# A two-layer hybrid decoder trunk on one core: the tile scheduler draws up the instruction order with its timeline machine model

## Chip, cores and metric

One core of one Trainium2 chip runs the whole kernel in one launch. The metric is the time on the device in microseconds (us), the median of several executions of the same program. Beside it stands one profiled execution, whose trace gives the start and the length of every instruction. Engines are named as in the profile: PE is TensorE's matmul, PEld its weight load, DVE is VectorE, ACT is ScalarE, POOL is GpSimd, SP is SyncE, which here issues every DMA. "SPq" is SP's queue of DMA issues.

## The reference

Sequence 1024, width 1024, batch 1, all float32. Layer 0 is retention with 4 heads, layer 1 is stick-breaking attention with 8 heads over a shared K and V.

```python
u = rms_norm(h, ret_norm_pre);  q, k, v, g = split(u @ ret_w_in)
q, k = rope(q), rope(k) * QK ** -0.5
o = retention_chunkwise(q, k, v)          # o_t = sum_{s<=t} gamma^(t-s) (q_t.k_s) v_s
o = layer_normalised(o) * silu(g)
h = h + rms_norm(o @ ret_w_out, ret_norm_post)
k_sh, v_sh = split(rms_norm(h, kv_norm) @ w_kv)
q, g = split(rms_norm(h, sb_norm_pre) @ sb_w_in)
o = stick_breaking(q, k_sh, v_sh) * silu(g)   # A = sigmoid(z) * prod of (1 - sigmoid(z)) between
h = h + rms_norm(o @ sb_w_out, sb_norm_post)
```

## The kernel before

The function `trunk` writes out the whole computation, transposed, with no loop at run time. The sequence is cut into two halves of 512 tokens, and the work runs through four phases: layer 0 on half 0, layer 0 on half 1, layer 1 on half 0, layer 1 on half 1. A phase has four units: a retention head (`AHead`) or a pair of attention heads (`CPair`).

Every product of float32 operands is done as three matmuls (`mm3`, lines 110 to 112) of operands that are split into a high and a low part. `split` makes the parts: ACT writes the high part (line 262, or 265 with a gain), then DVE writes the low part (line 263, or 266). Weights go through this too. `unit` loads a weight block of 128x1024 in two halves into buffers `wraw` (6 of 128x512) and splits it into `whl` (3 of 128x2x1024). A projection (`proj`) walks over 4 such weight blocks in 16 chunks of 6 matmuls each, so one weight block feeds 24 matmuls of 512 columns, and the next block is requested (`get(kk + 1)`) while the present one is used. Results gather in PSUM tiles `pma` and `pmb` (2 each); transposes and scores use `pz` (2), attention sums `po` (2).

The order in which the code issues its steps is written by hand: `merge` takes a main list (projection chunks) and side lists (scores, attention sums, gates, norms) and spreads the side steps over the main ones.

```python
def merge(main, *sides, nxt=None):
    done = [0] * len(sides)
    for i, m in enumerate(main):
        ...
        m()
        for k, (steps, lead, tail) in enumerate(sides):
            n = len(main) - lead - tail
            upto = min(len(steps), len(steps) * max(0, i + 1 - lead) // n)
            while done[k] < upto:
                steps[done[k]]()
                ...
```

That is not yet the order in which the engines run. When the block `with tile.TileContext(nc) as tc:` closes, the tile framework's scheduler runs the traced instructions through a model of the machine. Whenever an engine of the model is free, the scheduler gives it the earliest instruction in code order whose operands and buffers are ready in the model. It also hands out the buffers of each tag in that process, and puts in the semaphore waits. Each engine then runs its list strictly in that order on the chip; nothing is chosen again at run time. Without an argument the model is the framework's core simulator.

In the program that comes out before the change, TensorE's list has 8094 matmuls and transposes and steps back in code order at 8 places only. The other lists are far from code order already: DVE's 1947 instructions step back 505 times, ACT's 1526 324 times, SP's 1055 DMAs 196 times, POOL's 374 15 times.

Other lines that the prediction speaks of: 64 (every DMA's issue), 202 (`outproj` adds to a stored partial sum `y`), 504 and 508 (the sums of a product with seven multiplications in `vg`, which also forms sums of weights in lines 480 to 489), 694, 702 and 703 (`a_post`: residual add on POOL or DVE, square on ACT, sum on POOL), 806 (the gate's SiLU), 961 to 983 (`finish`, the last norm and the output).

## Time and profile before

| | |
|---|---|
| time, 3 runs | 1782.42, 1786.29 and 1787.54 us, median 1786.29 |
| profiled execution, first to last instruction | 1779.2 us |
| time of the profiled execution itself | not listed; by the three runs it lies 3.2 to 8.3 us above the span |
| instructions recorded | 23669 |
| PE, DVE, ACT, POOL busy | 97%, 67%, 46%, 16% of the span |
| mean granted TensorE clock | 0.996 of full speed |
| moved by DMA | 292.14 MB, mean 164 GB/s |

Busy time is the union of an engine's instructions; matmuls are pipelined, so their recorded lengths overlap, and what a stretch achieves is read better from the count of matmuls in it.

### The profile page before, as it was taken

The page shows a single profiled execution, that of the slowest core. Times are in us where ns is not written, and L with a number is a line of the kernel's source. Part 1 is how long each engine was busy: PE and PEld are TensorE (multiplying, and loading weights), DVE is VectorE, ACT ScalarE, POOL GpSimd, SP SyncE. Part 2 cuts the span into 40 slices and gives each one's busy share as a digit, 9 for nine tenths or more (in the row PEclk, how much of TensorE's full clock was granted, in tenths as well). Part 3 has the DMA queues.
Part 4 walks back from the last instruction along what each step waited for, and adds up shares of the span by engine and source line. Part 5 has one row for each costly group of instructions (what it writes and reads, how often), then busy time and mean ns, then how long its engine had stood idle before and what let it go on. Part 6 is the DMA issues. An engine that isn't in the chain of part 4 may idle for free.

```text
span 1779.2 us, 23669 instructions
## 1 busy us (share of the span) xinstructions
PE 1732.0 (97%) x8132; PEld 1432.3 (81%) x8132; DVE 1198.6 (67%) x1947; ACT 815.1 (46%) x1526; POOL 290.2 (16%) x377
## 2 busy tenths in 40 slices
PE   8999999999999999999999999999999999999997
PEld 6888788777788788877887888888778888888886
DVE  7756767789766868697485455556677456656675
ACT  6435545455445535364344343444445434444441
POOL 0210412232304320111130100000200010000003
PEclk9999999999999999999999999999999999999999
DMA  5225465557445646275664526345644433522243
GB/s 192 84 101 195 153 236 173 193 179 271 168 143 189 226 144 233 97 258 187 230 222 159 194 95 204 117 151 173 221 135 158 140 131 103 179 94 99 95 137 113
DMA packets 152553, 292.14 MB, mean 164 GB/s; under 512 B 17136, under 2 KB 19312, under 8 KB 152432
## 3 DMA queue, kind: packets, MB, share of 16 engines
q1 hardware_dynamic: 152432, 290.63, 48.2%
q8 instruction: 64, 1.05, 0.2%
q14 instruction: 57, 0.47, 0.1%
HBM read 233.93 MB, written 56.62 MB: 163 GB/s over the span
## 4 chain that ended last, share of the span: by engine, by line
PE 42%; issue 27%; DVE 16%; DMA 7%; POOL 4%; ACT 3%; SPq 1%; POOLq 0%; DVEq 0%; ACTq 0%
PE pma L111 6%; PE pmb L110 6%; PE pmb L111 6%; PE pmb L112 6%; PE pma L112 6%; PE pma L110 6%; DVE whl L263 3%; DMA wraw<-in_wts_dram 3%; PE po L111 2%; PE po L112 2%; PE po L110 2%; DVE sgn L838 1%; POOL small L622 1%; DMA y<-f 1%; DMA S<-in_xT_dram 1%
## 5 line engine op out<-in xcount | busy, mean ns | idle before, releaser
L263 DVE TENSOR_TENSOR whl<-wraw,whl 128x512 fp32r<-128x512 f32 x312 | 220.5, 735 | 67.8 <-ACT whl L262 67.2
L266 DVE SCALAR_TENSOR_TENSOR whl<-wraw,gn,whl 128x256 fp32r<-128x256 f32 (+1 forms) x256 | 153.5, 643 | 127.7 <-ACT whl L265 124.9
L262 ACT ACTIVATE whl<-wraw 128x512 fp32r<-128x512 f32 x312 | 183.5, 624 | 111.5 <-PE pmb L112 52.4
L265 ACT ACTIVATE whl<-wraw,gn 128x256 fp32r<-128x256 f32 (+1 forms) x256 | 143.1, 612 | 166.3 <-PE pmb L112 135.7
L110 PE MATMUL pmb<-xh,whl 128*128 128x512 f32 x384 | 153.1, 399 | 2.8 <-DVE sg L806 2.6
L110 PE MATMUL pma<-xh,whl 128*128 128x512 f32 x384 | 153.3, 399 | 1.2 <-DVE v L263 0.7
L112 PE MATMUL pmb<-xh,whl 128*128 128x512 f32 x384 | 150.3, 391 | 0.0
L112 PE MATMUL pma<-xh,whl 128*128 128x512 f32 x384 | 150.2, 391 | 0.0
L111 PE MATMUL pma<-xh,whl 128*128 128x512 f32 x384 | 149.8, 390 | 0.0
L111 PE MATMUL pmb<-xh,whl 128*128 128x512 f32 x384 | 149.7, 390 | 0.0
L836 POOL TENSOR_SCALAR_AFFINE_SELECT sgn<-sgn 128x128 f32<-128x128 f32 x64 | 24.8, 387 | 692.0 <-ACT sgn L831 580.1
L838 DVE TENSOR_TENSOR_SCAN sgn<-sgn 128x128 f32<-128x128 f32 (+3 forms) x64 | 89.1, 1393 | 45.0 <-POOL sgn L836 45.0
L263 DVE TENSOR_TENSOR AT<-pz,AT 128x512 fp32r<-128x512 f32 (+1 forms) x96 | 53.0, 553 | 72.3 <-ACT AT L262 71.9
L262 ACT ACTIVATE AT<-pz 128x512 fp32r<-128x512 f32 (+1 forms) x96 | 46.7, 487 | 111.5 <-PE pz L868 108.9
L110 PEld LDWEIGHTS pmb<-xh,whl 128*128 128x128 f32 x384 | 72.2, 188 | 18.5 <-DVE sg L806 5.3
L112 PEld LDWEIGHTS pmb<-xh,whl 128*128 128x128 f32 x384 | 72.1, 188 | 15.8
L112 PEld LDWEIGHTS pma<-xh,whl 128*128 128x128 f32 x384 | 72.1, 188 | 15.6
L110 PEld LDWEIGHTS pma<-xh,whl 128*128 128x128 f32 x384 | 72.2, 188 | 15.0 <-DVE v L263 1.1
L111 PEld LDWEIGHTS pmb<-xh,whl 128*128 128x128 f32 x384 | 72.2, 188 | 13.4
L111 PEld LDWEIGHTS pma<-xh,whl 128*128 128x128 f32 x384 | 72.3, 188 | 13.0
L110 PE MATMUL pma<-oT,whl 128*128 128x512 f32 x208 | 82.2, 395 | 0.5 <-DVE small L619 0.5
L111 PE MATMUL pma<-oT,whl 128*128 128x512 f32 x208 | 81.4, 392 | 1.2 <-DVE oT L263 1.2
(321 smaller groups left out, 4507.4 us busy)
## 6 DMA issues: line engine op xcount, KB each, us to landing
wraw<-in_wts_dram SPq DMA_DIRECT2D x624, 256.0 KB, 3.2
y<-f SPq DMA_DIRECT2D x120, 256.0 KB, 3.2
f<-y SPq DMA_DIRECT2D x88, 256.0 KB, 3.8
v<-v SPq DMA_DIRECT2D x16, 512.0 KB, 3.3
vo<-v SPq DMA_DIRECT2D x32, 256.0 KB, 2.9
A<-h SPq DMA_DIRECT2D x12, 512.0 KB, 4.3
st<-ko SPq DMA_DIRECT2D x8, 512.0 KB, 3.9
sg<-in_xT_dram SPq DMA_DIRECT2D x16, 256.0 KB, 2.9
```

What stands on the lines that cost most here:

```text
L110: MM(p, lh, rh, start=start, stop=False, **kw)
L111: MM(p, lh, rl, start=False, stop=False, **kw)
L112: MM(p, ll, rh, start=False, stop=stop, **kw)
L262: A_.activation(dst[0], src, AF.Copy)
L263: V.tensor_tensor(dst[1], src, f32(dst[0]), ALU.subtract)
L265: A_.activation(dst[0], src, AF.Copy, scale=scale)
L266: V.scalar_tensor_tensor(dst[1], src, scale, f32(dst[0]), ALU.mult, ALU.subtract)
L622: G.tensor_tensor(r[:], r[:], mhalf[:, 0:1], ALU.pow)
L836: G.affine_select(n[:, dg], n[:, dg], [[-1, 128]], ALU.is_gt, 1.0, base=0, channel_multiplier=1)
L838: V.tensor_tensor_scan(n[:, :W][:, ::-1], n[:, :W][:, ::-1], n[:, :W][:, ::-1], 1.0, ALU.mult, ALU.bypass)
```

## The change

The scheduler's machine model is replaced: it now runs the traced instructions through the framework's timeline simulator, which models each engine's sequencer, queue and data path, the DMA engines and the semaphores' travel as separate devices. No instruction of the computation, no tile, buffer count or hint in the code differs. All five instruction lists, TensorE's among them, are drawn up anew, as are the buffers that each tile gets and the semaphore waits that follow from the order.

```diff
-    with tile.TileContext(nc) as tc:
+    with tile.TileContext(nc, schedule_with_timeline_sim=True) as tc:
         trunk(tc, *args)
```

## The prediction, made before the changed kernel was run

> **What bounds the kernel now.** I read the busy shares first, then who TensorE waits for, then one stretch where it starves.
>
> ```profile
> span 1779.2 us, 23669 instructions
> PE 1732.0 (97%) x8132; PEld 1432.3 (81%) x8132; DVE 1198.6 (67%) x1947; ACT 815.1 (46%) x1526; POOL 290.2 (16%) x377
> PE   8999999999999999999999999999999999999997
> PEclk9999999999999999999999999999999999999999
> ```
>
> TensorE is the bound from the second slice to the last but one. The change moves none of its work away, so its 1732.0 us stay, and the order of the lists can only act on the 47.2 us of the span (1779.2 - 1732.0) in which it does nothing. The list of TensorE's waits says what those are; it has 25 rows, of which these are the longest and the last:
>
> ```profile
> PE pma L110 <- ACT whl L262: 8.2, 3, 6.5
> PE pz L666 <- DVE oT L263: 3.2, 2, 1.8
> PE pz L868 <- DVE AT L263: 3.1, 3, 2.0
> PE pmb L110 <- DVE sg L806: 2.6, 5, 1.2
> PE pma L111 <- DVE whl L263: 2.5, 4, 0.9
> PE pz L967 <- DVE acc L961: 2.2, 1, 2.2
> PE pz L977 <- DVE f L972: 1.6, 1, 1.6
> PE pz L236 <- DVE acc L352: 0.2, 1, 0.2
> 1770.37 0.71 PE L977 MATMUL pz<-f,ones 128*128 128x256 f32 x2 [1.55 <-DVE f L972]
> ```
>
> The columns are total us, times, longest us. All 25 rows add up to 38.6 us. Three parts of it no order can remove: the 6.5 us at the start (the first weight block must land and be split), and the 2.2 and 1.6 us of the last norm, where no other matmul is left. After the last matmul (1770.37 + 0.71) another 8.1 us of output follow. What stays is 38.6 - 6.5 - 2.2 - 1.6 = **28.3 us** of short waits in mid-span, none above 2.0 us, spread over all phases. In each, TensorE's list stood at an instruction whose operand was late, though later ones in code order may have been ready.
>
> **What one bad place in the order costs.** The thickest cluster lies at 575 to 597 us. Here is the count of matmuls in it beside the next stretch, and what ACT, POOL, SP and TensorE did:
>
> ```profile
> core 0: us, PE busy (x) PEld busy (x) DVE busy (x) ACT busy (x) POOL busy (x), PEclk, DMA share, GB/s
> 575.00:597.00 22.00, 17.18 (x63) 12.28 (x62) 17.18 (x27) 10.15 (x18) 4.32 (x2) 0.92 0.70 241
> 597.00:617.00 20.00, 20.00 (x90) 16.40 (x89) 20.00 (x30) 13.11 (x23) 5.73 (x4) 1.00 0.70 234
> 576.44 6.55 SPq L64 DMA_DIRECT2D wraw<-in_wts_dram  x9
> 583.98 0.43 SPq L64 DMA_DIRECT2D vo<-in_xT_dram  x1
> 587.47 3.04 POOL L694 TENSOR_TENSOR vo<-vo,vo 128x512 f32<-128x512 f32 x1 [12.50 <-DMA vo<-in_xT_dram]
> 590.54 0.63 ACT L702 ACTIVATE vo<-vo 128x512 f32<-128x512 f32 x1 [2.32 <-POOL vo L694]
> 591.08 0.61 ACT L262 ACTIVATE whl<-S 128x512 fp32r<-128x512 f32 x1
> 591.75 0.49 PE L110 MATMUL pma<-whl,A 128*128 128x512 f32 x1 [0.91 <-ACT whl L262]
> ```
>
> The square of a residual tile (line 702) stands in ACT's list ahead of a weight split (line 262). Its input came late: the load of x was issued behind nine weight loads, and POOL waited 12.50 us for it. ACT then held still 2.32 us with the split behind it, and TensorE waited for the split. The next stretch does 90 matmuls in 20.00 us, 0.222 us each. At that pace 22 us hold 99, and 63 were done: 36 x 0.222 = **8.0 us lost**, against 4.8 us that the waits of this stretch come to (1.7 + 1.5 + 1.1 + 0.5):
>
> ```profile
> PE pma L110 <- ACT whl L262: 1.7, 2, 0.9
> PE pma L111 <- DVE whl L263: 1.5, 2, 0.9
> PE po L111 <- DVE whl L263: 1.1, 1, 1.1
> PE pmb L111 <- DVE whl L263: 0.5, 1, 0.5
> 594.00 0.63 PE L110 MATMUL pma<-whl,A 128*128 128x512 f32 x1
> 594.42 0.63 PE L111 MATMUL pma<-whl,A 128*128 128x512 f32 x1
> 598.03 0.39 PE L110 MATMUL pmb<-whl,xh 128*128 128x512 f32 x1
> 598.26 0.40 PE L111 MATMUL pmb<-whl,xh 128*128 128x512 f32 x1
> ```
>
> The difference is the clock: at 594 us matmuls start 0.42 us apart, at 598 us 0.23 us, and the granted clock of the stretch is 0.92. So a cluster of waits, none above 1.1 us, brought a spell at half clock after it.
> The Trainium skill ("TensorE: Matmul & The Clock Gate", Part 1) says that the clock halves after an idle window of about 3.4 us. By its letter these waits of 1.1 us at most cost their 4.8 us alone; this trace disagrees, and the measured 8.0 us decides.
>
> **The change part by part.**
> *Work.* Every instruction, operand and DMA stays, so busy times stay: 0 us.
>
> *TensorE's list.* Before the change it is almost code order. A model in which operands come later than in the old one will see gaps and fill them with later matmuls; a matmul put forward by some tenths of a microsecond costs nothing, as the work is the same. It gains where the model sees a wait that the chip has, and where other work is ready. Bounds: 0, and the 28.3 - 4.8 = 23.5 us outside the cluster. Chain waits such as transposes behind DVE (lines 666, 868) have projection matmuls beside them, so a filler often exists, but a model need not place a wait of 1 us where the chip has it. I take two fifths: **-9 us**.
>
> *ACT's, DVE's and POOL's lists.* The cluster is a list that put a late operand first. A model with DMA engines as a device of their own should land that load later and put the split first. Bounds 0 and -8.0; I take **-5 us**, as the load's delay came from a queue of nine loads, which such a model should show.
>
> *SP's list.* All 1055 DMAs can change places, and SP's queue blocks as a whole:
>
> ```profile
> SPq L64 <- DVE whl L263: 375.0, 234, 15.6
> SPq L64 <- DVE f L202: 89.4, 61, 13.7
> ACT whl L265 <- PE pmb L112: 135.7, 54, 5.2
> ```
>
> The first row is harmless: SP waits for a `wraw` buffer to be split. The second is a store of a partial sum that waits up to 13.7 us for DVE, with weight loads queued behind it. The cover is the weights in hand: a block feeds 24 matmuls, 24 x 0.222 = 5.3 us, and 3 split plus 3 loaded blocks are up to 32 us. The third row shows that the cover is there: ACT waits for TensorE to give a `whl` buffer back, not the other way round. I cost SP's list at 0 with that cover; where a block's four stages are empty, as at the start of a head, it is part of the next term.
>
> *New waits.* Lists drawn by a model of the machine bring waits wherever model and chip differ. Nothing in this trace shows the new ones. Bounds: 0 (the new lists have no waits of their own), and for the upper end the price of the nearest row, 8.0 us, for each new bad place. Lists made by the old model have 28.3 us of waits and one cluster; two thirds of a cluster is my value: **+5 us**. Below nothing is excluded, as the gains are counted already.
>
> Sum: -9 - 5 + 5 = **-9 us**. The span of 1779.2 us would become 1770. The profiled execution's own time is not listed; the median of the three runs is 7.1 us above the span. Against that median the forecast is 1786.3 - 9 = **1777 us**.
>
> **The rivals.**
> *The new lists block on late operands (slower).* The mechanism is the cluster's, in new places: ACT's or DVE's list puts an instruction first whose operand comes over DMA or POOL later on the chip than in the model, and a weight split or a PSUM read stands behind it. For it speaks that POOL's additions are erratic (3.04 us above, 1.30 in a row below) and that a load's landing hangs on the queue ahead; a model that fills every gap leaves less slack where it errs. Against it speaks ACT's 46% and DVE's 67%, which absorb much. Price 8.0 us a place; with the gain of 14 us and none of the +5, it decides from the third place on: 3 x 8.0 - 14 = +10. One such place in every phase and one more (5 places): 5 x 8.0 - 14 = +26, **1812 us**.
>
> *TensorE's list stays as it is (no change).* If in the new model too TensorE is never short of ready work, its list keeps code order, the other lists shift inside their slack, and the 28.3 us stay with other names: **1785 us**, between 1781 and 1791. For it speaks that only 8 places of 8094 deviate now; against it, that the chip itself has 25 kinds of waits.
>
> *POOL and DVE in each other's way (slower).* A DVE split beside a POOL addition takes longer:
>
> ```profile
> 591.73 1.35 DVE L263 TENSOR_TENSOR whl<-S,whl 128x512 fp32r<-128x512 f32 x1 [2.36 <-ACT whl L262]
> 591.25 1.27 POOL L703 TENSOR_TENSOR acc<-acc,vo 128x512 f32<-128x512 f32 x1 [0.74 <-ACT vo L702]
> L263 DVE TENSOR_TENSOR whl<-wraw,whl x312: 650/683/1789, 6.5 to 1718.3; 128x512 fp32r<-128x512 f32 x156
> 573.66 1.30 POOL L703 TENSOR_TENSOR acc<-acc,vo 128x512 f32<-128x512 f32 x1 [0.74 <-ACT vo L702]
> ```
>
> 1.35 against a median of 0.683 us. Were all of POOL's 290.2 us laid beside DVE work that is free of it now, DVE would have 1198.6 + 290.2 = 1489 us, 84%, still under TensorE's 97%. It would bind only in single stretches like the second of the table above (DVE 20.00 of 20.00); at 0.67 us more for each of the 30 DVE instructions there, +20 us, **1806 us**.
> The Trainium skill ("SBUF — State Buffer", the summary of rules) says that of two such operations the second one blocks until the first is done; by that rule the whole overlap is lost, which these rows bear out in size (0.67 us of 1.27).
>
> **How the numbers follow.** A difference of 0.3% (5.4 us) is about what a measurement of this kernel can tell from none. Gaps partly filled: 0.43, its own range 1754 to 1781. No change: 0.20, of which 0.02 ends faster and 0.01 slower. Blocking on late operands: 0.35. POOL and DVE: 0.02. So faster 0.43 + 0.02 = 0.45, same 0.17, slower 0.38. The likeliest gives 1777. Range: below, everything recoverable, 28.3 + 3.2 (the half clock in the cluster) = 31.5, is 1755; I put 1754. Above, six bad places on top of a net gain of 9: 48 - 9 = +39, 1825. Outside I leave 0.05 below and 0.13 above.
>
> **What would show it.** Right: TensorE's waits in mid-span fall from 28.3 to about 15 us, the stretch around 583 to 597 us runs at full clock, busy times stay within 1%, and TensorE's list steps back in code order at many more than 8 places. Wrong: a new long row "PE <- ACT whl" or "PE <- DVE", longest above 3 us, with ACT or DVE idle just before it on a DMA or POOL; more slices with PEclk below 9; or PE waits that keep their sum and only change names. The forecast fails if the model's idea of when operands come is worse than the old one's, since the gain is bounded by 31.5 us and the loss by nothing.

## Result and the profile after

| | before | after |
|---|---|---|
| median time, 4 runs each | 1786.07 us (1782.42 to 1787.54) | 1814.18 us (1810.50 to 1815.43) |
| profiled span | 1779.2 us | 1808.8 us |
| end of the last matmul | 1771.1 us | 1800.4 us |

The ratio is 1.0162, 95% interval 1.0145 to 1.0178: the changed kernel is slower by 28 us. The profiled execution took 1810.5 us, 1.7 us more than its span. First the busy shares of the page after:

```profile
span 1808.8 us, 23788 instructions
PE 1743.8 (96%) x8132; PEld 1439.8 (80%) x8132; DVE 1201.8 (66%) x1947; ACT 806.8 (45%) x1526; POOL 292.2 (16%) x377
```

Each engine does as many instructions as before (the 119 more records, 23788 against 23669, are semaphore instructions), DVE and ACT are busy to within about 1% as long as before, and the 29.6 us of span lie with TensorE: 11.8 us in which it is busy longer with the same 8132 matmuls (1743.8 - 1732.0) and 17.8 us more in which it does nothing (65.0 against 47.2). The first part goes with the clock, as the last section works out, the second is the waits. TensorE's list of waits has 22 rows, among them these (total us, times, longest us):

```profile
PE pmb L111 <- DVE whl L263: 7.2, 9, 1.8
PE pma L111 <- DVE whl L263: 5.2, 8, 1.6
PE po L110 <- ACT sgn L635: 4.6, 1, 4.6
```

All rows add up to 56.5 us. Without the start (6.8) and the last norm (3.7 and 1.6), 44.4 us of waits lie in mid-span, where before had 28.3. They don't lie evenly. Set against the trace of before matmul by matmul, TensorE falls behind in a few lumps and runs level between them. The eight stretches in which it loses most:

```profile
core 0: us, PE busy (x) PEld busy (x) DVE busy (x) ACT busy (x) POOL busy (x), PEclk, DMA share, GB/s
31.00:45.00 14.00, 8.02 (x21) 5.22 (x19) 12.73 (x20) 7.32 (x13) 0.00 (x0) 0.63 0.12 37
412.00:424.00 12.00, 7.43 (x28) 5.77 (x26) 12.00 (x23) 5.11 (x10) 2.65 (x3) 0.72 0.84 283
549.00:557.00 8.00, 5.56 (x16) 3.77 (x17) 8.00 (x17) 2.26 (x4) 4.69 (x3) 0.79 0.22 68
590.00:622.00 32.00, 25.31 (x96) 18.12 (x95) 29.61 (x37) 15.03 (x26) 15.76 (x8) 0.95 0.73 250
663.00:672.00 9.00, 5.93 (x21) 3.80 (x20) 8.85 (x12) 3.98 (x7) 4.86 (x4) 0.83 0.40 132
770.00:776.00 6.00, 3.15 (x11) 1.83 (x10) 6.00 (x10) 3.66 (x7) 3.57 (x3) 0.90 0.26 87
794.00:826.00 32.00, 27.53 (x113) 20.13 (x111) 29.54 (x47) 17.32 (x32) 1.22 (x2) 1.00 0.67 226
1398.00:1412.00 14.00, 8.24 (x30) 5.43 (x30) 12.40 (x12) 8.29 (x18) 3.56 (x6) 0.79 0.28 94
```

Read the count of matmuls behind the busy time of PE. At the 0.222 us per matmul of an undisturbed stretch the eight rows would hold 63, 54, 36, 144, 40, 27, 144 and 63; the matmuls missing cost 9.3, 5.8, 4.4, 10.7, 4.3, 3.6, 6.9 and 7.3 us, together 52 us. The fourth row is the old cluster, which cost 8.0 us before. So some 44 us are new, and some 15 us were gained elsewhere (both rough, as short matmuls are counted like long ones). In all eight rows DVE is busy for 88% of the stretch or more (12.40 of 14.00 is the least), in three of them without a break: TensorE starves while DVE works. A busy DVE alone is no sign, though: before the change it was busy for 20.00 of 20.00 us at 597 us with TensorE full. The question is what stands in DVE's list ahead of the step that TensorE needs.

**What stands in front.** From the timelines of the first lump, after:

```profile
29.85 0.39 PE L254 MATMUL pz<-sgn,onesr 128*128 128x512 f32 x1
31.21 0.39 PE L254 MATMUL pz<-sgn,onesr 128*128 128x512 f32 x1
31.64 0.60 ACT L256 ACTIVATE acc<-pz 128x512 f32<-128x512 f32 x1
32.35 1.40 DVE L308 SCALAR_TENSOR_TENSOR S<-S,gn,acc 128x512 f32<-128x512 f32 x2
...
36.32 1.41 DVE L308 SCALAR_TENSOR_TENSOR ko<-ko,gn,acc 128x512 f32<-128x512 f32 x2
37.65 0.74 DVE L266 SCALAR_TENSOR_TENSOR v<-pmb,small,v 128x512 fp32r<-128x512 f32 x1
34.42 1.22 PE L110 MATMUL pma<-xh,whl 128*128 128x512 f32 x2 [2.59 <-ACT xh L262]
38.44 0.80 PE L110 MATMUL pmb<-xh,whl 128*128 128x512 f32 x1 [2.38 <-DVE v L266]
```

and at the same work before:

```profile
26.09 0.62 PE L254 MATMUL pz<-sgn,onesr 128*128 128x512 f32 x2
27.56 1.41 DVE L308 SCALAR_TENSOR_TENSOR S<-S,gn,acc 128x512 f32<-128x512 f32 x2
28.89 0.75 DVE L308 SCALAR_TENSOR_TENSOR ko<-ko,gn,acc 128x512 f32<-128x512 f32 x1
32.72 1.40 DVE L266 SCALAR_TENSOR_TENSOR v<-pmb,small,v 128x512 fp32r<-128x512 f32 x2
```

Two things happen here. On TensorE, the two matmuls that make the row of the norm (line 254) ran one behind the other at 26.09 us; now they stand among the projection matmuls into `pmb`, at 29.85 and 31.21 us. Line 308, which scales the input by that row, could start only when ACT had copied it (31.64 us). Then DVE's new list takes all eight of its instructions in one block (four rows, 32.35 to 37.65), and the read of `pmb` that frees the buffer, and the splits of `xh`, stand behind it. Before, three of them went first, and both reads of `pmb` (32.72) stood ahead of the other five.

The second lump shows the same in a chain of small steps, the layer norm of a head (lines 617 to 635):

```profile
412.00 0.18 DVE L617 BATCH_NORM_AGGREGATE small<-small 128x2 f32<-128x6 f32 x1
417.00 0.15 DVE L619 TENSOR_SCALAR small<-small 128x1 f32<-128x1 f32 x1
417.90 0.78 ACT L635 ACTIVATE sgn<-po,small,small 128x512 f32<-128x512 f32 x1 [0.68 <-POOL small L623]
418.73 0.80 PE L110 MATMUL po<-v,vo 128*128 128x512 f32 x1 [4.57 <-ACT sgn L635]
```

and the first two of these steps before:

```profile
400.26 0.17 DVE L617 BATCH_NORM_AGGREGATE small<-small 128x2 f32<-128x6 f32 x1
400.93 0.14 DVE L619 TENSOR_SCALAR small<-small 128x1 f32<-128x1 f32 x1
```

Between the two steps DVE now does eight instructions of 128x512 (two of them weight splits, two of line 308), so line 619 comes 5.0 us after line 617 instead of 0.67 us, and TensorE stands 4.57 us for the end of that chain. The Trainium skill ("TensorE: Matmul & The Clock Gate", the table of specifications) calls the queues of ScalarE, VectorE and GpSimd strictly first in, first out; these rows agree: nothing on DVE passed the eight instructions.

The third lump is the plainest case. DVE forms the rotated q and k from `pmb` (lines 400 to 403), and line 403 is the read that frees the buffer. After:

```profile
549.44 1.59 POOL L404 TENSOR_TENSOR f<-f,f 128x512 f32<-128x512 f32 x1 [0.92 <-DVE f L402]
549.81 1.77 DVE L263 TENSOR_TENSOR whl<-wraw,whl 128x512 fp32r<-128x512 f32 x1
551.50 0.68 DVE L403 TENSOR_TENSOR f<-pmb,tab 128x512 f32<-128x512 f32 x1
552.23 0.50 PE L110 MATMUL pmb<-oT,whl 128*128 128x512 f32 x1 [1.73 <-DVE f L403]
```

and before:

```profile
544.84 0.68 DVE L403 TENSOR_TENSOR f<-pmb,tab 128x512 f32<-128x512 f32 x1
545.44 1.46 DVE L263 TENSOR_TENSOR whl<-wraw,whl 128x512 fp32r<-128x512 f32 x1
```

A weight split (and one of `qk`, at 549.21 us) now stands in front of line 403 instead of behind it, and TensorE waits 1.73 us for the read. The fifth lump has the same two rows, at 665.99 and 667.68 us.

### The profile page after: what moved, and what is told of

It is laid out like the page before. It is cut to its first block, busy times and chain, and to the rows that moved or that the text cites. A ratio compares the mean times of both kernels' runs of the same rounds, so it can differ in the third digit from the quotient of the medians.

```text
span 1808.8 us, 23788 instructions
## 1 busy us (share of the span) xinstructions
PE 1743.8 (96%) x8132; PEld 1439.8 (80%) x8132; DVE 1201.8 (66%) x1947; ACT 806.8 (45%) x1526; POOL 292.2 (16%) x377
## 4 chain that ended last, share of the span: by engine, by line
PE 71%; DVE 11%; issue 8%; DMA 7%; ACT 1%; POOL 1%; SPq 0%; DVEq 0%; POOLq 0%; ACTq 0%
PE pma L111 10%; PE pma L112 10%; PE pma L110 10%; PE pmb L111 9%; PE pmb L112 9%; PE pmb L110 9%; DVE whl L263 3%; DMA wraw<-in_wts_dram 3%; PE po L111 3%; PE po L112 3%; PE po L110 3%; DMA sg<-in_xT_dram 1%; PE pz L868 1%; PE pz L112 1%; PE pz L111 1%
## 5 line engine op out<-in xcount | busy, mean ns | idle before, releaser
L263 DVE TENSOR_TENSOR whl<-wraw,whl 128x512 fp32r<-128x512 f32 x312 | 216.7, 730 | 88.1 <-ACT whl L262 87.8
L262 ACT ACTIVATE whl<-wraw 128x512 fp32r<-128x512 f32 x312 | 179.5, 624 | 174.4 <-PE pmb L112 105.3
L836 POOL TENSOR_SCALAR_AFFINE_SELECT sgn<-sgn 128x128 f32<-128x128 f32 x64 | 29.8, 466 | 692.9 <-ACT sgn L831 581.7
```

The lines of the kernel that those rows point to most:

```text
L262: A_.activation(dst[0], src, AF.Copy)
L263: V.tensor_tensor(dst[1], src, f32(dst[0]), ALU.subtract)
L836: G.affine_select(n[:, dg], n[:, dg], [[-1, 128]], ALU.is_gt, 1.0, base=0, channel_multiplier=1)
```

## The experiments

The theories. *TensorE's list*: its new order loses (theory A in the expectations). *The other lists*: those of DVE, ACT or SP lose. *Buffers and waits*: the new assignment of buffers and semaphores loses, whatever the order. Later, as theory E: *overtaking* — bulk work that is ready (weight splits, projection matmuls) is put ahead of a chain's next step whose operand comes some tenths later, and the chain pays at every engine it crosses.

The tool of most experiments is a function that ties an engine to a given list, by a dependency of issue order alone, without a wait:

```python
def in_order(tc, nc, engine, order):      # order None: code order
    ...
    for a, b in zip(names, names[1:]):
        tc.add_manual_dep(traced[b], a, mybir.DependencyInfo(mybir.DependencyClass.NoSync, ...))
```

The calls stand behind `trunk(tc, *args)`; `B_` is a list of before, `A_` one of after. The kernel before measured 1784.3, 1784.8 and 1784.7 us in the three batches; every ratio is to it.

**1. TensorE alone tied to code order.**

```diff
     trunk(tc, *args)          # timeline model
+    in_order(tc, nc, "PE", None)
```

> The timeline model draws up the lists of DVE, ACT, POOL and SP; TensorE's list is tied to the order in which the code issues its 8094 steps. Theory A (the loss comes from TensorE's new list: small matmuls of a chain, such as the row of the norm on line 254, are overtaken by projection matmuls, and what hangs on them comes late): the time returns to that of before, 1780 to 1792 us, the granted clock to 0.995, and the starved stretches at 31 to 44, 410 to 425 and 1400 us vanish. Theory B (the loss comes from the lists of DVE and ACT, where instructions of 0.15 us such as line 619 stand behind 5 us of splits): it stays above 1805 us.

1819.05 us, ratio 1.0193 (1.0172 to 1.0213). With TensorE's list as good as the old one nothing is recovered, so the theory that its list alone loses falls. The other lists lose by themselves. The row of TensorE's waits that grew most is for a weight split's low part, 0.8 us in before; the longest single wait is in a chain through DVE, 0.2 us in before:

```profile
PE pmb L111 <- DVE whl L263: 12.5, 9, 2.5
PE pz L868 <- DVE A L839: 8.8, 5, 5.6
```

**2. Only TensorE's list of after, the rest by the old model.**

```diff
     trunk(tc, *args)          # old model
+    in_order(tc, nc, "PE", A_PE)
```

> The other half: the old model draws up DVE, ACT, POOL and SP around TensorE's list of the changed kernel, taken over matmul by matmul. Theory A: 1805 to 1820 us, with the starved stretches and spells at half clock in the same places. Theory B: the old lists of the others heal most of it, below 1796 us.

1820.01 us, ratio 1.0199 (1.0179 to 1.0220). TensorE's list loses by itself as well. With run 1, each side alone is at least as dear as the whole.

**3. The timeline model, all five engines tied to before's lists.**

```diff
     trunk(tc, *args)          # timeline model
+    for e in ("PE", "DVE", "Activation", "Pool", "SP"): in_order(tc, nc, e, B_[e])
```

> The timeline model is used, but all five lists are tied to those of the kernel before; only the buffers handed out and the waits put in can still differ. If the order is all that matters: 1786 us within 0.3%. If the new model's buffers or waits cost something by themselves: above 1792 us.

1783.89 us (10 runs), ratio 0.9999 (0.9986 to 1.0012). With the order held, the new model's buffers (570 of 2849 tiles lie at other addresses) cost nothing that these runs can tell. The changed kernel has 1131 tiles at other addresses and 119 semaphore instructions more; those follow from its order and can't be had without it, but run 10 has 885 and 92 and is 4.6 us above before.

**4. On TensorE no matmul may pass an earlier one into `pz` or `po`.**

```diff
+    chains_first(tc, nc)      # projections (pma, pmb) don't pass chains (pz, po) on PE
```

> The timeline model with one rule for TensorE: no matmul passes one that the code issued before it and that writes pz or po (transposes, scores, norms, attention sums); projection matmuls may still change places among themselves (205 steps back in code order against 448). Theory A in its narrow form (what costs is overtaking the chains): 1780 to 1792 us, as with TensorE in code order. Rival C (what costs is that projection matmuls of several PSUM banks are interleaved, so that banks close late): it stays above 1800 us.

1809.26 us, ratio 1.0141 (1.0120 to 1.0161). A rule on TensorE alone gives back little, if anything: its interval overlaps that of the change (1.0145 to 1.0178). The time is the one that rival C forecast; run 10 speaks against that rival, as it leaves projection matmuls free to change places among themselves.

**5 to 8. One engine's list by the timeline model, the other four tied to before's.**

```diff
     trunk(tc, *args)          # timeline model; run 5 (PE free) shown, 6 to 8 likewise
+    for e in ("DVE", "Activation", "Pool", "SP"): in_order(tc, nc, e, B_[e])
```

TensorE free:

> Four lists tied to those of before, TensorE's alone drawn up by the timeline model (5445 of 8094 matmuls stand elsewhere, by 8.8 places in the mean). Theory A (filling gaps on TensorE costs by itself, since a matmul that hands work to DVE is overtaken): 1795 to 1815 us, with lost stretches at 545 to 565, 640 to 660 and 1380 to 1400 us of before. Theory D (a new list costs only together with other new lists, as the engines then disagree): within 0.3% of 1785 us.

DVE free:

> DVE's list alone drawn up by the timeline model (843 of 1945 instructions stand elsewhere). Theory B (DVE is busy without a break in the stretches that lose, so its list decides there what TensorE gets, and the model ranks it worse): 1795 to 1815 us, with losses near 390 to 430, 700 and 1700 us. Theory D: within 0.3% of 1785 us.

ACT free:

> ACT's list alone drawn up by the timeline model (457 of 1525 instructions stand elsewhere). ACT is busy 46% of the span, so theories A and B both expect 1780 to 1792 us; if ACT's list carries the loss, above 1795 us.

SP free:

> SP's list of DMA issues alone drawn up by the timeline model (312 of 1055 DMAs stand elsewhere). Theories A and B expect 1780 to 1790 us, as the weights in hand cover the shifts; the prediction's term for SP was 0.

| free | median us | ratio (95%) | over before |
|---|---|---|---|
| TensorE | 1815.84 | 1.0175 (1.0155 to 1.0196) | +31 |
| DVE | 1817.37 | 1.0184 (1.0160 to 1.0208) | +33 |
| ACT | 1801.58 | 1.0097 (1.0080 to 1.0114) | +17 |
| SP, 8 runs | 1791.55 | 1.0043 (1.0028 to 1.0057) | +7 |

Each of the four lists loses alone (POOL's was not run); together they would make 88 us, while the change costs 28. A likely reason, not tested, is that lists of one model share its idea of when things happen, and against before's lists each is out of step. The times of runs 5, 6 and 8 lie somewhat above the ranges expected. With DVE free, TensorE's row of waits for a weight split's low part grows from 2.5 us in before to 18.7; there it is the bulk itself that comes late, which overtaking doesn't describe:

```profile
PE pma L111 <- DVE whl L263: 18.7, 12, 4.1
```

With ACT free, two timelines show one lump of run 7, ACT's squares of the next input and TensorE's wait:

```profile
204.50 0.63 ACT L380 ACTIVATE sg<-sg 128x512 f32<-128x512 f32 x1 [2.63 <-DMA sg<-in_xT_dram]
207.37 0.63 ACT L380 ACTIVATE sg<-sg 128x512 f32<-128x512 f32 x1 [2.24 <-DMA sg<-in_xT_dram]
210.53 0.78 ACT L635 ACTIVATE sgn<-po,small,small 128x512 f32<-128x512 f32 x1
216.29 1.12 PE L666 MATMUL pz<-ident,sgn 128*128 128x128 f32 x4 [4.52 <-DVE oT L263]
```

Here it is a late operand: ACT stands 2.63 and 2.24 us for loads of x with the norm's step (line 635) queued behind, which before ran at 206.34 us.

**9. ACT free as in run 7, with four pairs of neighbours swapped back: the norm's step ahead of the squares.**

```diff
+    in_order(tc, nc, "Activation", ORDER_SQUARES_AND_NORMS)   # lines 378, 380, 635 only
```

> As the run with ACT's list alone drawn up by the timeline model (1801.6 us), but on ACT the head's normalisations (line 635) and the squares of the next half's statistics (lines 378, 380) keep the order of before: four pairs of neighbours in ACT's list change places, nothing else. If the squares, whose operand comes by DMA, hold up the normalisation that TensorE's transposes wait for: the losses at 206 to 229 us (5.6 us) and 315 to 342 us (4.2 us) go, 1790 to 1794 us. If not: 1800 to 1803 us.

1797.32 us, ratio 1.0066 (1.0044 to 1.0087): about 4 of the 17 us, less than expected. In the profiled runs the lump near 330 us went, the one near 215 us shrank from 5.6 to 3.6 us, and a new one of 3.8 us stood near 450 us. The late load explains part of ACT's loss; the rest is open.

**10. Timeline model for all lists, but bulk passes no chain's step that it doesn't pass in before's list.**

```diff
+    for e in ("DVE", "Activation", "PE"): no_new_overtaking(tc, nc, e, B_[e])
+    # bulk: matmuls into pma/pmb on PE, splits into whl on ACT and DVE
```

> The timeline model draws up all lists under one rule for PE, ACT and DVE: bulk work (matmuls into pma and pmb, the splits that write whl) may not pass an instruction of a chain that it did not pass in the kernel before. Theory E (the new lists lose because bulk work overtakes the chains that feed TensorE: in the changed kernel the tiles pz and po come 11 places later in TensorE's list in the mean): 1783 to 1793 us. Rival F (any order that rests on the timeline model loses, wherever it differs): above 1800 us.

1789.29 us (10 runs), ratio 1.0024 (1.0010 to 1.0039). 3042 matmuls still stand elsewhere than before, yet some 85% of the loss is gone (1.0024 against 1.0162). That the rule only brings the lists nearer to before's is not the reason: in run 1, which lost 35 us, 109 matmuls and 1010 of DVE's instructions stand elsewhere, here 3042 and 891. Six windows of this run; the last two lie where its own longest lumps are:

```profile
core 0: us, PE busy (x) PEld busy (x) DVE busy (x) ACT busy (x) POOL busy (x), PEclk, DMA share, GB/s
31.00:45.00 14.00, 11.27 (x43) 8.84 (x42) 12.02 (x20) 6.07 (x12) 0.00 (x0) 0.88 0.19 61
549.00:557.00 8.00, 8.00 (x37) 6.64 (x36) 4.68 (x8) 3.79 (x7) 0.41 (x1) 1.00 0.70 225
412.00:424.00 12.00, 12.00 (x57) 9.91 (x56) 10.66 (x19) 5.71 (x10) 0.00 (x0) 1.00 0.86 284
1398.00:1412.00 14.00, 14.00 (x63) 11.53 (x63) 6.73 (x12) 7.09 (x14) 0.00 (x0) 1.00 0.37 127
575.00:607.00 32.00, 25.14 (x94) 18.10 (x92) 29.41 (x37) 13.68 (x24) 14.56 (x8) 0.89 0.72 244
779.00:822.00 43.00, 39.71 (x161) 30.49 (x160) 40.69 (x68) 23.63 (x43) 4.35 (x6) 0.96 0.59 193
```

Three are full again. Matmul by matmul, nothing is lost any more at the work of five lumps (the second, third, fifth, sixth and eighth). Three stay. In the first, 43 matmuls run where 63 fit, 4.4 us: line 254 is back at 26.90 us, but DVE still takes line 308's eight in one block, from 28.37 to 33.68 us, since the rule counts only weight splits as bulk:

```profile
28.37 1.41 DVE L308 SCALAR_TENSOR_TENSOR S<-S,gn,acc 128x512 f32<-128x512 f32 x2
35.69 0.50 PE L110 MATMUL pma<-xh,whl 128*128 128x512 f32 x1 [2.73 <-DVE v L266]
```

Run 6, where DVE's list alone is new, has the same block and 42 matmuls in that window. So the block makes about half of the first lump's 9.3 us. The old cluster (fifth row) lacks 50 matmuls, 11.1 us, and the stretch near 800 us (last row) 33, 7.3 us: as much as with the change. In both TensorE waits for the low part of weight splits (5.8 and 4.8 us), so for bulk, which this rule holds back. What the rule covers came back, and what it leaves out stayed; that the run is only 4.6 us above before is a net, with gains elsewhere.

**11. The reverse: the chains keep before's order among themselves, bulk is free to overtake.**

```diff
+    for e in ("DVE", "Activation", "PE"): chains_as_given(tc, nc, e, B_[e])
```

> The reverse: the instructions of the chains on PE, ACT and DVE keep among themselves the order of the kernel before, and bulk work may overtake them wherever the timeline model likes. Theory E: 1800 to 1820 us, as with the change. If what costs is the order among the chains' own instructions: below 1792 us.

1859.24 us, ratio 1.0414 (1.0386 to 1.0442), 75 us above before. Keeping the order within the chains gives nothing back, so it is not what was lost; with run 10, the freedom of bulk against them is. That it is 45 us worse than the change was not expected (1800 to 1820 us), and why stays open.

**12. Before's five lists, with 85 matmuls moved up into waits that the trace of before shows, each only where the trace shows its operands ready.**

```diff
     trunk(tc, *args)          # old model
+    in_order(tc, nc, "PE", B_PE_WITH_85_MOVED_UP)
+    for e in ("DVE", "Activation", "Pool", "SP"): in_order(tc, nc, e, B_[e])
```

> All five lists of the kernel before, but 85 of TensorE's matmuls are moved up by 2 to 14 places into waits of 0.2 to 2.0 us that the trace of before shows, and only matmuls whose operands that trace shows as ready. The waits that they cover come to 14.7 us. If filling gaps on TensorE is harmless by itself and the model's idea of readiness is what fails: 1770 to 1778 us. If moving matmuls ahead of chains costs whatever it is based on: 1785 us or more.

1775.11 us (6 runs, 1774.39 to 1777.78), ratio 0.9948 (0.9929 to 0.9968): faster than the kernel before by 9.6 us. In the finished list 83 matmuls stand earlier, by up to 20 places. The window of the old cluster:

```profile
575.00:597.00 22.00, 18.24 (x75) 14.02 (x76) 19.19 (x30) 12.14 (x22) 3.43 (x3) 1.00 0.75 242
```

The cluster holds 75 matmuls instead of 63, at full clock. Filling TensorE's gaps can be worth what the prediction hoped of it, if the list is drawn from measured waits. That the 9.6 us are so near the -9 of that term is luck: the list is another, and so are the moves.

## Why the prediction was wrong, point by point

*What held.* Busy times stayed within about 1%. TensorE's list steps back in code order at 448 places instead of 8; 5346 of its 8094 instructions stand elsewhere, and the mean shift over all of them is 13 places. Gaps were filled in places: between 320 and 345 us TensorE gained some 6 us on before; score matmuls now run between the two matmuls of a norm's row, which stood together behind DVE. After:

```profile
338.50 0.39 PE L254 MATMUL pz<-sgn,onesr 128*128 128x512 f32 x1
338.72 0.39 PE L110 MATMUL pz<-qk 128*128 128x512 f32 x1
```

against before:

```profile
336.92 1.23 PE L254 MATMUL pz<-sgn,onesr 128*128 128x512 f32 x2 [2.01 <-DVE sgn L247]
```

*The step that failed: that a matmul put forward by some tenths of a microsecond costs nothing (TensorE's list, -9), with the price of new waits put at +5.* By the count of lumps the gains came to some 15 us, near the 14 of the sum, though the cluster, which was to give 5 of them, got worse; the new lumps cost some 44 us instead of 5. A matmul put forward costs what it overtakes. In the new list the matmuls of the chains (`pz`, `po`) stand 11.7 and 11.5 places later in the mean, those of the projections (`pma`, `pmb`) 4.4 and 4.2 earlier. 11.7 places are 11.7 x 0.222 = 2.6 us, and the chain crosses DVE, whose list lets bulk pass too, at 0.6 us a weight split. Run 5 puts the list at +31 against before's other lists. That such a gain is there to be had is no error: run 12 got 9.6 us from filling.

*ACT's, DVE's and POOL's lists, -5.* The cluster was to be cured. It stayed, and grew from 8.0 to 10.7 us; in 590 to 622 us the list of waits has the old row, larger:

```profile
ACT vo L702 <- POOL vo L694: 9.0, 2, 5.4
```

Beyond that, DVE's and ACT's lists alone cost 33 and 17 us (runs 6 and 7). That DVE's 67% would absorb a bad place was wrong: in the lumps it is busy for 88% or more, and an average says nothing of them.

*SP's list, 0.* Alone it costs 7 us (run 8). Its profiled execution, the slowest of the eight with 1796.48 us, has its largest lump, 6.9 us, near 930 us. What in SP's order makes it was not separated.

*New waits, +5.* The term was taken from the waits and the one cluster that lists of the old model have, and these say nothing of lists by another model: seven new lumps and a dearer cluster, some 44 us.

*The rival that came nearest* was "the new lists block on late operands", with 5 places at 8.0 us less 14, 1812 us. The direction, the arithmetic by places and the spells at half clock were right: seven new places at 3.6 to 9.3 us, the cluster 2.7 us dearer, some 15 us of gains. That the sum comes so near to 1814.18 us is in part luck, as there are more and cheaper places. Its mechanism was right only in part. ACT idle behind POOL or a load is seen in the old cluster, in run 7 and, with 2.3 us as the longest wait, in the third, fifth and sixth lump; but there and in the others DVE is busy, which the prediction's signs ("DVE idle just before") would have missed.

*POOL and DVE in each other's way* played no part in the first lump: POOL does nothing there (0.00). In the third and fifth it has a share: the split ahead of line 403 took 1.77 us beside a POOL addition, against a median of 0.683 us in before, so that 1.1 of the 1.73 us that TensorE waited go with it. Run 10 had both lumps back by the order alone. The prediction set its 0.67 us against the addition's 1.27 us; the two instructions that it shows overlap for 0.79 us only (591.73 to 592.52), so nearly all of the overlap was lost.

*What stays open.* Why the model sees bulk ready first: it may think a chain's steps take too long, or that loads land too soon; no run separated these. Run 10 was never combined with a rule for line 308, run 9 gave back a quarter of ACT's loss only, and what makes weight splits late in the old cluster and near 800 us was not tested.

## What to carry to other kernels

A scheduler that always takes what is ready can fill a helper engine with bulk just ahead of the short step that the bound engine needs next, as here; look for stretches where the bound engine starves while a helper is busy, and ask there what stands in front of the chain's step. If bulk is kept from passing chains, do it on every engine at once: on TensorE alone the rule gave back little (run 4), on three engines 85% of the loss (run 10), though not more than the old order had. If single waits are to be filled, take the places and the ready operands from a measured trace: 85 moves gained 9.6 us here, while a list with 5346 matmuls elsewhere, with the four other new lists, lost 28.

## What the runs showed of the hardware

Clusters of short waits can halve the clock. In the stretch at 549 us the granted clock is 0.79 with 1.7 us as the longest of three waits, which add up to 2.4 us. Before the last norm the trace after has seven spells at half clock, of 3.4 us (four), 6.8 us (two) and 10.2 us, 37 us together and one in each of the stretches shown but that at 794 us (granted clock 1.00), where before had two of 3.4 us. 31 us more at half the clock can lose up to 15 us of matmul time, and TensorE is busy 11.8 us longer with the same matmuls: two fifths of the loss. The Trainium skill ("TensorE: Matmul & The Clock Gate", Part 1) describes a free-running window of about 3.4 us, and a clock that halves after at least one window of idleness. The lengths here agree with the window, being 3.4 us or twice or three times that; that a whole window must be idle these runs do not bear out.

The traces say more. In the trace after, the spells start whole multiples of 3.413 us apart (the first at 34.1, the last at 1406.3 us, 402 steps). Lay steps of that length over the whole trace: in the step before each of the seven starts TensorE was idle for 1.75 us or more in total, and in no other step at full clock for more than 1.6 us. In before the two starts follow 1.8 and 2.0 us, and no other step holds more than 1.5; run 12, with waits of 1.5, 1.4 and 1.1 us in its cluster, has no step above 1.5 us and no spell there. So in these traces about half a step of idleness, in however many pieces, goes with a halved clock. Between the start and the last norm of all fourteen traces, 69 of 75 spells start after a step with 1.7 us or more, and only 14 of 7045 other steps at full clock held as much; the six spells that start after 1.2 to 1.6 us are not explained, and the ends of matmuls in a trace are modelled.
